# Small loads on ACT's queue, w_mod products between the transposes, two rows as single-column matmuls

## The chip, the core and the metric

The kernel runs on one core of one Trainium2 chip. The metric is the device time of one execution in microseconds (us), here the median of 3 runs. The core has a matrix engine (TensorE, in the profile PE, with its weight loads shown as PEld), two elementwise engines (VectorE = DVE, ScalarE = ACT), GpSimd (POOL, almost unused here) and SyncE (SP). SP and ACT can both issue DMA transfers; each engine goes through its instructions in program order.

## The reference

Two layers of a mixer on x of 256 tokens by 2048 channels, batch 1. What matters for this change is the very beginning of layer 0:

```
c_act = silu(c)
mod = c_act @ w_mod[0] + b_mod[0]            # 2048 -> 3 * 2048
shift, scale, gate = split(mod, 3)
h = rms_norm(x, g_norm) * (1 + scale) + shift
proj = h @ w_in[0]                           # 2048 -> 15424
```

Behind it come retention, latent attention, their projections, the merge, the output projection, the second layer with the same shapes, and a last RMS norm. All of it is float32.

## The kernel before, in words

Tokens are 256, so one operand of the large products is always 256 columns wide or two blocks of 128 rows. Weights stream once from memory in pieces of 128 x 1024 (512 KB). Each piece is split by ACT (`hi`, L240) and DVE (`lo`, L241) into two float32r parts, and three matmuls (hi·hi, hi·lo, lo·hi; L273 and L276) replace one float32 product.

The change lies in the opening stretch, `start()` (L510 to L559) and the loads ahead of it (L164 to L205). `start()` makes the first four of sixteen 128-row blocks of h, so that the first columns of w_in can be multiplied before the rest of w_mod has been read. Its steps:

- Small loads: the constants `cst` (identity and tables, 67 KB, L165), five row vectors `rows` (b_mod, g_norm, g_cq, g_ckv, c; L182) that PE turns into columns (L185), and `posi`, the positions broadcast to 128 partitions (L197). SiLU of c gives `cact` (L194).
- x in four tiles of 512 KB (`xin`, L205), each squared and summed by ACT (L518). DVE makes the rotary angles from `posi` (L216 to L224). Then the reciprocal root (L305 to L310).
- PE transposes x in eight pairs of blocks (L530), and ACT copies each pair from a PSUM buffer into `xT` (L532). Four such buffers (`aux_tile`) rotate.
- `spread` (L327 to L337) turns the reciprocal root into a row `r` on all partitions, and DVE scales four blocks of x with it (`xh0`, L444).
- The first 512 columns of shift and scale take sixteen pieces of w_mod (`wmod`, 512 KB, two 128-row blocks each), loaded with the scale half first (L391). The scale half is multiplied on PE with `cact` as the stationary operand, one result row of 512 columns (L540, sixteen matmuls). The shift half is accumulated on DVE, one instruction for each block of rows (L347, L349, sixteen in all), and PE then sums over the partitions with a vector of ones (`mod_sum`, L355).
- `make_amul` (L424) forms (1 + scale)·g; DVE multiplies xh0 by it (L549); ACT adds the shift and rounds (`hi`, L556), DVE makes `lo` (L557). With that PE starts on w_in (L273).

In `start()` the order on PE, DVE and ACT is the order of the code (`manual_schedule`). Elsewhere a scheduler chooses. DMA transfers carry one of eight completion semaphores, DMAHW0 to DMAHW7, handed out in rotation over all queues in the order in which the scheduler takes the transfers; a transfer that gets a semaphore again waits, on its own queue, until the earlier one that carried it has landed.

Of the kernel before, what the change touches and what calls it, by code (L numbers as in the profile page):

```python
# [13 lines left out]
AF = mybir.ActivationFunctionType  # L14
ALU = mybir.AluOpType
AX = mybir.AxisListType

P = 128
S = 256
D = 2048  # L20
KT = D // P
# [87 lines left out]
def trunk(ctx: ExitStack, tc: tile.TileContext, x, c, positions, w_mod, b_mod, g_norm, w_in, g_cq,  # L109
          g_ckv, w_uq, w_ukv, w_ret_proj, w_mla_proj, w_out, g_final, consts, decay, out):  # L110
    nc = tc.nc
    V, A, T, DMA = nc.vector, nc.scalar, nc.tensor, nc.sync
# [14 lines left out]
    def aux_tile():  # L127
        return paux.tile([P, 512], F32, name="aux", tag="aux")

    def tmp_tile():  # L130
        return tp.tile([P, 512], F32, name="tmp", tag="tmp")

    def small(n):
        return sp.tile([P, 16], F32, name="small", tag="small")[:, :n]

    def quarter(name, dtype=F32):
        return big.tile([P, 1024], dtype, name=name, tag="quarter")

    def blocks(name):

        return quarter(name).rearrange("p (a b) -> p a b", b=S)
# [20 lines left out]
            return [u[:, kt % 2, cols] for u in self.pair(kt // 2)]  # L162

    cst = cp.tile([P, K_COLS], F32, name="cst")  # L164
    DMA.dma_start(cst, consts)  # L165
    ident = cst[:, K_ID : K_ID + P]
    ones = cp.tile([P, P], F32, name="ones")
    V.memset(ones, 1.0)
# [6 lines left out]
    def vectors(l):  # L175
        rows = tp.tile([P, P], F32, name="rows", tag="tmp")
        put = [(b_mod[l], 48), (g_norm[l], 16), (g_cq[l], 4), (g_ckv[l], 4)]
        if l == 0:
            put.append((c[0], 16))
        r0 = 0  # L180
        for src, n in put:
            DMA.dma_start(rows[r0 : r0 + n, :], src.rearrange("(r q) -> r q", q=P))  # L182
            r0 += n
        ps = aux_tile()
        T.transpose(ps[:, :r0], rows[:r0, :], ident[:r0, :r0])  # L185
        V.tensor_copy(vec[l][:, :r0], ps[:, :r0])

    vectors(0)
    bm = [v[:, 0:48] for v in vec]
    gn = [v[:, 48:64] for v in vec]  # L190
    gcq = [v[:, 64:68] for v in vec]
    gckv = [v[:, 68:72] for v in vec]
    cact = cp.tile([P, KT], F32, name="cact")
    A.activation(cact, vec[0][:, 72:88], AF.Silu)  # L194

    posi = tp.tile([P, S], I32, name="posi", tag="tmp")
    DMA.dma_start(posi, positions.broadcast_to([P, S]))  # L197
    pos = dp.tile([P, S], F32, name="pos", tag="dtab")


# [60 lines left out]
    def mm3(o, a, b, start, stop):  # L261

        T.matmul(o, a[0], b[0], start=start, stop=False, skip_group_check=True)  # L263
        T.matmul(o, a[0], b[1], start=False, stop=False, skip_group_check=True)  # L264
        T.matmul(o, a[1], b[0], start=False, stop=stop, skip_group_check=True)  # L265
# [36 lines left out]
    def rsqrt_small(v, n):  # L302

        s, y, t = small(n), small(n), small(n)
        A.activation(s, v, AF.Sqrt)  # L305
        V.reciprocal(y, s)
        V.tensor_tensor(t, y, y, ALU.mult)
        V.tensor_tensor(t, t, v, ALU.mult)
        V.tensor_scalar(t, t, -0.5, 1.5, ALU.mult, ALU.add)
        V.tensor_tensor(y, y, t, ALU.mult)  # L310
        return y
# [16 lines left out]
    def spread(y, r=None):  # L328

        tt = tmp_tile()  # L330
        pr = aux_tile()
        for t in range(2):
            V.tensor_scalar(tt[:, t * P : (t + 1) * P], ident, y[:, t : t + 1], None, ALU.mult)
            T.matmul(pr[:, t * P : (t + 1) * P], ones, tt[:, t * P : (t + 1) * P], start=True, stop=True)
        r = tt[:, S : 2 * S] if r is None else r
        A.activation(r, pr[:, :S], AF.Copy)
        return r  # L337

    mods = [cp.tile([P, 48 if l < DEPTH - 1 else 32], F32, name=f"mod{l}") for l in range(DEPTH)]
    amul = [cp.tile([P, KT], F32, name=f"amul{l}") for l in range(DEPTH)]  # L340
# [3 lines left out]
    def mod_rows(acc, w, k0, nk):  # L344
        for k in range(nk):
            if k0 + k == 0:
                V.tensor_scalar(acc, w[:, k, :], cact[:, 0:1], None, ALU.mult)  # L347
            else:
                V.scalar_tensor_tensor(acc, w[:, k, :], cact[:, k0 + k : k0 + k + 1], acc, ALU.mult, ALU.add)  # L349

    def mod_sum(l, m0, ng, pieces, one):
        ps = aux_tile()
        for b in range(ng):
            for i, piece in enumerate(pieces):
                T.matmul(ps[:, b : b + 1], piece[:, b * P : (b + 1) * P], one, start=i == 0, stop=i == len(pieces) - 1)  # L355
        V.tensor_tensor(mods[l][:, m0 : m0 + ng], ps[:, :ng], bm[l][:, m0 : m0 + ng], ALU.add)
# [29 lines left out]
    def mod_fetch(w, l, m0, k0, ng):  # L386

        n = ng * P
        w = w.rearrange("p (k n) -> p k n", n=n)
        nd = 1024 // n  # L390
        DMA.dma_start(w, w_mod[l, k0 * P : (k0 + nd) * P, m0 * P : m0 * P + n].rearrange("(k p) n -> p k n", p=P))  # L391
        return w
# [30 lines left out]
    def make_amul(l, k, n):  # L423
        V.scalar_tensor_tensor(amul[l][:, k : k + n], mods[l][:, 16 + k : 16 + k + n], 1.0,  # L424
                               gn[l][:, k : k + n], ALU.add, ALU.mult)
# [17 lines left out]
    def normalise(dst, k, r):  # L443
        V.tensor_tensor(dst, xT[:, k : k + 2, :], r.unsqueeze(1).broadcast_to([P, 2, S]), ALU.mult)  # L444
        return dst
# [60 lines left out]
    def start():  # L506

        ng = GROUPS[0][0][1]
        nd = 8 // ng
        ws = {(i, k): mod_fetch(quarter("wmod"), 0, 16 * i, k, ng) for i in (1, 0) for k in range(0, KT, nd)}  # L510
        ss = small(4).rearrange("p (q t) -> p q t", q=2)
        extra, room = quarter("extra"), quarter("room")
        row, acc = extra[:, : ng * P], extra[:, 512 : 512 + ng * P]
        xh0, hh = blocks("xh0"), Pairs("h")
        with tc.manual_schedule(engines={ENG.PE, ENG.DVE, ENG.Activation}):
            for q in range(2):
                for t in range(2):
                    A.activation(room, xin[t][q], AF.Square, accum_out=ss[:, q, t : t + 1])  # L518
            rotary = rotary_tables(quarter("angle"))
            next(rotary)  # L520
            v = small(2)
            V.tensor_tensor(v, ss[:, 0, :], ss[:, 1, :], ALU.add)
            V.tensor_scalar(v, v, 1.0 / D, EPS, ALU.mult, ALU.add)
            y = rsqrt_small(v, 2)
            for pair in range(KT // 2):
                ps = aux_tile()
                for a in range(2):
                    for t in range(2):
                        f = (2 * pair + a) * P
                        T.transpose(ps[:, a * S + t * P : a * S + (t + 1) * P],  # L530
                                    xin[t][f // 1024][:, f % 1024 : f % 1024 + P], ident)
                A.activation(xT[:, 2 * pair : 2 * pair + 2, :].rearrange("p a b -> p (a b)"), ps, AF.Copy)  # L532
            r = spread(y, dp.tile([P, S], F32, name="r0", tag="dtab"))
            for k in range(0, ng, 2):
                normalise(xh0[:, k : k + 2, :], k, r)
            next(rotary, None)
            pr = aux_tile()
            for k0 in range(0, KT, nd):
                for k in range(nd):
                    T.matmul(pr[0:1, : ng * P], cact[:, k0 + k : k0 + k + 1], ws[1, k0][:, k, :], start=k0 + k == 0,  # L540
                             stop=k0 + k == KT - 1)
            for k0 in range(0, KT - nd, nd):
                mod_rows(acc, ws[0, k0], k0, nd)
            A.activation(row[0:1, :], pr[0:1, : ng * P], AF.Copy)
            mod_sum(0, 16, ng, [row[0:1, :]], ones[0:1, 0:1])
            make_amul(0, 0, ng)
            mod_rows(acc, ws[0, KT - nd], KT - nd, nd)
            for k in range(ng):
                V.tensor_scalar(xh0[:, k, :], xh0[:, k, :], amul[0][:, k : k + 1], None, ALU.mult)  # L549
            first = [w_in[0, k0 * P : (k0 + 2) * P, n : n + 512] for n in (C_RQ, C_RK) for k0 in range(0, ng, 2)]  # L550
            prepared.append(load_split(first[0], 2, 512, early=True))
            mod_sum(0, 0, ng, [acc], ones[:, 0:1])
            for k in range(ng):
                hi, lo = hh.block(k)
                shift = mods[0][:, k : k + 1]
                A.activation(hi, xh0[:, k, :], AF.Identity, bias=shift)  # L556
                V.scalar_tensor_tensor(lo, xh0[:, k, :], shift, hi.bitcast(F32), ALU.add, ALU.subtract)  # L557
            prepared.extend(load_split(src, 2, 512, early=True) for src in first[1:HP])
        return r, hh  # L559
# [444 lines left out]
    r = u = None  # L1004
    for l in range(DEPTH):
        r, u = layer(l, r, u)
# [22 lines left out]
```

## Time and profile before

| what | value |
|---|---|
| median of 3 runs | 2056.74 us (2056.7 to 2057.08) |
| profiled execution | 2057.32 us |
| its span, first to last instruction | 2055.5 us |
| PE busy | 2025.8 us, 99% of the span |
| DVE, ACT busy | 1483.6 us (72%), 1061.7 us (52%) |
| first w_in matmul | 39.93 us after the start of the span |

The span is one execution as the hardware profiler saw it; 1.8 us of the execution lie outside it. A busy share is an average over the whole span, so what happens in its first 45 us has to be read from the timeline of that stretch, and the granted clock from the table of stretches.

### The profile page before, as it was taken

The numbers are of one execution on the slowest core, as the hardware profiler recorded it, in microseconds if no ns is written. First come the engines' busy times: TensorE is split into PE (matmuls) and PEld (weight loads), VectorE is DVE, ScalarE is ACT, GpSimd is POOL, SyncE is SP. The second block draws the span as 40 slices with busy tenths as digits, with TensorE's granted clock in tenths as the row PEclk, the third lists the DMA queues.
The fourth block names the chain that finished last, engine by engine and source line by source line (L and its number), as shares of the span: only waits on it lengthen the run. The fifth ranks groups of instructions, "written<-read, shape, count | busy, mean of one in ns | idle before, by whom it ended". The sixth has DMA issues, their size and how long they took to land.

```text
span 2055.5 us, 31773 instructions
## 1 busy us (share of the span) xinstructions
PE 2025.8 (99%) x12414; PEld 1802.8 (88%) x12414; DVE 1483.6 (72%) x2082; ACT 1061.7 (52%) x1489; POOL 0.2 (0%) x4
## 2 busy tenths in 40 slices
PE   7999999999999999999999999999999999999998
PEld 4888888998899998889998888889889999988887
DVE  5799986778777777775577776568776877765574
ACT  4554355654456664444454464456544666644453
POOL 0000000000000000000000000000000000000000
PEclk9999999999999999999999999999999999999999
DMA  8998966567866668875569966665677666666572
GB/s 315 321 310 274 308 198 194 159 191 259 302 191 195 195 187 274 281 267 185 182 196 333 326 209 189 194 180 156 198 238 223 205 185 195 208 224 192 190 243 90
DMA packets 251222, 460.59 MB, mean 224 GB/s; under 512 B 18464, under 2 KB 68032, under 8 KB 251072
## 3 DMA queue, kind: packets, MB, share of 16 engines
q1 hardware_dynamic: 251072, 458.57, 69.8%
q8 instruction: 97, 1.59, 0.3%
q14 instruction: 53, 0.43, 0.1%
HBM read 456.41 MB, written 2.10 MB: 223 GB/s over the span
## 4 chain that ended last, share of the span: by engine, by line
PE 94%; DMA 3%; DVE 2%; ACT 1%; issue 1%; SPq 0%; ACTq 0%; DVEq 0%
PE acc L273 57%; PE acc L276 28%; DMA ring<-in_w_mod 2%; DMA wmod<-in_w_mod 1%; PE aux L264 1%; PE aux L265 1%; PE aux L263 1%; PE acc L263 1%; PE acc L264 1%; PE acc L265 1%; DVE extra L349 0%; PE aux L880 0%; ACT whl L240 0%; PE aux L721 0%; PE aux L846 0%
## 5 line engine op out<-in xcount | busy, mean ns | idle before, releaser
L240 ACT ACTIVATE whl<-wst 128x1024 fp32r<-128x1024 f32 (+1 forms) x708 | 709.0, 1007 | 805.0 <-PE acc L276 699.1
L241 DVE TENSOR_TENSOR whl<-wst,whl 128x1024 fp32r<-128x1024 f32 (+1 forms) x708 | 814.2, 1156 | 378.3 <-ACT whl L240 374.3
L273 PE MATMUL acc<-whl,h 128*128 128x512 f32 x2048 | 515.4, 392 | 0.0
L273 PEld LDWEIGHTS acc<-whl,h 128*128 128x128 f32 x2048 | 381.4, 188 | 77.1
L273 PE MATMUL acc<-h,whl 128*128 128x256 f32 x2432 | 328.1, 285 | 4.0 <-ACT h L240 2.4
L273 PEld LDWEIGHTS acc<-h,whl 128*128 128x128 f32 x2432 | 307.8, 192 | 6.3 <-ACT h L240 3.2
L276 PE MATMUL acc<-whl,h 128*128 128x512 f32 x1024 | 279.6, 392 | 0.4 <-DVE whl L241 0.4
L273 PE MATMUL acc<-whl,z 128*128 128x512 f32 x1024 | 254.8, 390 | 1.2 <-ACT whl L240 1.2
L273 PEld LDWEIGHTS acc<-whl,z 128*128 128x128 f32 x1024 | 191.8, 188 | 41.1 <-ACT whl L240 1.6
L276 PEld LDWEIGHTS acc<-whl,h 128*128 128x128 f32 x1024 | 190.9, 188 | 39.4 <-DVE whl L241 1.0
L276 PE MATMUL acc<-h,whl 128*128 128x256 f32 x1216 | 176.3, 284 | 0.0
L276 PEld LDWEIGHTS acc<-h,whl 128*128 128x128 f32 x1216 | 158.7, 192 | 0.1
L276 PE MATMUL acc<-whl,z 128*128 128x512 f32 x512 | 137.1, 390 | 0.0
L400 DVE SCALAR_TENSOR_TENSOR macc<-ring,cact,macc 128x1024 f32<-128x1024 f32 x75 | 96.1, 1281 | 35.7 <-DMA ring<-in_w_mod 35.2
L400 DVE SCALAR_TENSOR_TENSOR macc<-wst,cact,macc 128x1024 f32<-128x1024 f32 x90 | 115.0, 1278 | 0.0
L276 PEld LDWEIGHTS acc<-whl,z 128*128 128x128 f32 x512 | 96.0, 188 | 20.1 <-DVE whl L241 0.2
L273 PE MATMUL acc<-c,whl 128*128 128x256 f32 x640 | 100.2, 288 | 0.0
L273 PEld LDWEIGHTS acc<-c,whl 128*128 128x128 f32 x640 | 85.9, 191 | 0.2
L273 PE MATMUL acc<-m,whl 128*128 128x256 f32 x512 | 67.3, 283 | 0.0
L273 PEld LDWEIGHTS acc<-m,whl 128*128 128x128 f32 x512 | 64.0, 192 | 0.1
L276 PE MATMUL acc<-c,whl 128*128 128x256 f32 x320 | 57.6, 285 | 0.0
L273 PE MATMUL acc<-whl,m 128*128 128x512 f32 (+1 forms) x256 | 56.5, 365 | 0.0
(256 smaller groups left out, 1880.1 us busy)
## 6 DMA issues: line engine op xcount, KB each, us to landing
wst<-in_w_in SPq DMA_DIRECT2D x416, 512.0 KB, 4.4
wst<-in_w_mod SPq DMA_DIRECT2D x96, 512.0 KB, 4.7
ring<-in_w_mod SPq DMA_DIRECT2D x80, 512.0 KB, 5.3
wst<-in_w_ret_proj SPq DMA_DIRECT2D x64, 512.0 KB, 4.8
wst<-in_w_mla_proj SPq DMA_DIRECT2D x64, 512.0 KB, 4.4
wst<-in_w_out SPq DMA_DIRECT2D x64, 512.0 KB, 3.7
wst<-in_w_ukv SPq DMA_DIRECT2D x32, 512.0 KB, 4.3
wst<-in_w_uq SPq DMA_DIRECT2D x32, 384.0 KB, 4.2
```

The costliest lines, as they stand in the source:

```text
L240: A.activation(hi, src, AF.Copy)
L241: return V.tensor_tensor(lo, src, hi.bitcast(F32), ALU.subtract)
L263: T.matmul(o, a[0], b[0], start=start, stop=False, skip_group_check=True)
L264: T.matmul(o, a[0], b[1], start=False, stop=False, skip_group_check=True)
L265: T.matmul(o, a[1], b[0], start=False, stop=stop, skip_group_check=True)
L273: T.matmul(o, x, y, start=start and i == 0, stop=False, skip_group_check=True)
L276: T.matmul(o, x, y, start=False, stop=stop, skip_group_check=True)
L400: V.scalar_tensor_tensor(macc, w, cact[:, k : k + 1], macc, ALU.mult, ALU.add)
```

## The change

Three things change. The constants, the five row vectors of layer 0 and the positions are issued by ACT, and SP begins with x. Eight of the sixteen scale products move up between the last four pairs of transposes; the PSUM buffer of their sum is therefore held from before the first pair. DVE's shift rows stop after fourteen of sixteen, the scale is applied to xh0 after ten of them, and the last two rows are multiplied on PE, with the 128 x 128 blocks of w_mod as the stationary operand and one column of `cact` moving, into the same PSUM columns as the sum over partitions.

```
-    DMA.dma_start(cst, consts)
+    A.dma_start(cst, consts)
...
-            DMA.dma_start(rows[r0 : r0 + n, :], src.rearrange("(r q) -> r q", q=P))
+            (DMA if l else A).dma_start(rows[r0 : r0 + n, :], src.rearrange("(r q) -> r q", q=P))
...
-    DMA.dma_start(posi, positions.broadcast_to([P, S]))
+    A.dma_start(posi, positions.broadcast_to([P, S]))
...
+            pr = aux_tile()
+
+            def scale_rows(k0):
+                for k in range(k0, k0 + nd):
+                    T.matmul(pr[0:1, : ng * P], cact[:, k : k + 1], ws[1, k0][:, k - k0, :], start=k == 0, stop=k == KT - 1)
+
             for pair in range(KT // 2):
...
+                if pair >= KT // 4:
+                    scale_rows((pair - KT // 4) * nd)
...
-            pr = aux_tile()
-            for k0 in range(0, KT, nd):
-                for k in range(nd):
-                    T.matmul(pr[0:1, : ng * P], cact[:, k0 + k : k0 + k + 1], ws[1, k0][:, k, :], start=k0 + k == 0,
-                             stop=k0 + k == KT - 1)
+            for k0 in range(KT // 4 * nd, KT, nd):
+                scale_rows(k0)
             for k0 in range(0, KT - nd, nd):
                 mod_rows(acc, ws[0, k0], k0, nd)
-            A.activation(row[0:1, :], pr[0:1, : ng * P], AF.Copy)
-            mod_sum(0, 16, ng, [row[0:1, :]], ones[0:1, 0:1])
-            make_amul(0, 0, ng)
-            mod_rows(acc, ws[0, KT - nd], KT - nd, nd)
-            for k in range(ng):
-                V.tensor_scalar(xh0[:, k, :], xh0[:, k, :], amul[0][:, k : k + 1], None, ALU.mult)
+                if k0 == KT // 2:
+                    A.activation(row[0:1, :], pr[0:1, : ng * P], AF.Copy)
+                    mod_sum(0, 16, ng, [row[0:1, :]], ones[0:1, 0:1])
+                    make_amul(0, 0, ng)
+                    for k in range(ng):
+                        V.tensor_scalar(xh0[:, k, :], xh0[:, k, :], amul[0][:, k : k + 1], None, ALU.mult)
...
-            mod_sum(0, 0, ng, [acc], ones[:, 0:1])
+            ps = aux_tile()
+            for b in range(ng):
+                T.matmul(ps[:, b : b + 1], acc[:, b * P : (b + 1) * P], ones[:, 0:1], start=b == 0, stop=False,
+                         skip_group_check=True)
+            for k in range(KT - nd, KT):
+                for b in range(ng):
+                    T.matmul(ps[:, b : b + 1], ws[0, KT - nd][:, k - KT + nd, b * P : (b + 1) * P], cact[:, k : k + 1],
+                             start=False, stop=k == KT - 1, skip_group_check=True)
+            V.tensor_tensor(mods[0][:, 0:ng], ps[:, :ng], bm[0][:, 0:ng], ALU.add)
```

The head of ACT's instructions after the change, with the semaphores that each waits for (before, ACT began with the table load, and the seven transfers stood first on SP without a wait):

```order
L165 DMA cst<-in_consts 128x134
L182 DMA rows<-in_b_mod 48x128
L182 DMA rows<-in_g_norm 16x128
L182 DMA rows<-in_g_cq 4x128
L182 DMA rows<-in_g_ckv 4x128 [waits DMAHW1_49]
L182 DMA rows<-in_c 16x128 [waits DMAHW3_49]
L197 DMA posi<-in_positions 128x256 [waits DMAHW5_49]
L194 ACT_TABLE_LOAD
L194 ACTIVATE cact<-vec_88 128x16 [waits DVE_49]
```

The seven transfers moved from SP to ACT. The rotation now runs over both queues: cst has DMAHW0, the first tile of x DMAHW1, the second DMAHW2, b_mod DMAHW3, the third tile DMAHW4, g_norm DMAHW5, the fourth tile DMAHW6, g_cq DMAHW7, the first piece of w_mod DMAHW0, and g_ckv, the tenth transfer, DMAHW1 again.

PE from its first instruction to the first w_in matmuls, before:

```order
L185 MATMUL aux<-cst,rows 128x88
L530 MATMUL aux<-cst,xin 128x128 x32
L334 MATMUL aux<-tmp,ones 128x128 x2
L540 MATMUL aux<-wmod,cact 1x512 x16
L355 MATMUL aux<-ones,extra 128x1 x8
L273 MATMUL acc<-h,whl 128x256 x16
```

The same stretch of PE after:

```order
L536 MATMUL aux<-cst,xin 128x128 x20
L529 MATMUL aux<-wmod,cact 1x512 x2
L536 MATMUL aux<-cst,xin 128x128 x4
L529 MATMUL aux<-wmod,cact 1x512 x2
L334 MATMUL aux<-tmp,ones 128x128 x2
L529 MATMUL aux<-wmod,cact 1x512 x8
L355 MATMUL aux<-ones,extra 128x1 x4
L559 MATMUL aux<-ones,extra 128x1 x4
L563 MATMUL aux<-cact,wmod 128x1 x8
L273 MATMUL acc<-h,whl 128x256 x16
```

The four transposes and two products alternate four times in all. Eight scale products moved ahead of the two matmuls of `spread` (L334), and eight single-column matmuls (L563) came in between the sum over partitions (L559) and w_in.

DVE from `xh0` to the first `lo` of h, before:

```order
L444 TENSOR_TENSOR xh_157<-xT,r_236 128x512 x2
L347 TENSOR_SCALAR extra<-wmod,cact 128x512
L349 SCALAR_TENSOR_TENSOR extra<-wmod,cact,extra 128x512 x13
L356 TENSOR_TENSOR mod_117<-aux,vec_88 128x4
L424 SCALAR_TENSOR_TENSOR amul_119<-mod_117,vec_88 128x4
L349 SCALAR_TENSOR_TENSOR extra<-wmod,cact,extra 128x512 x2
L549 TENSOR_SCALAR xh_157<-xh_157,amul_119 128x256 x4
L241 TENSOR_TENSOR whl<-wst,whl 128x1024
L557 SCALAR_TENSOR_TENSOR h<-xh_157,mod_117,h 128x256 x4
```

The same stretch of DVE after:

```order
L444 TENSOR_TENSOR xh_157<-xT,r_245 128x512 x2
L347 TENSOR_SCALAR extra<-wmod,cact 128x512
L349 SCALAR_TENSOR_TENSOR extra<-wmod,cact,extra 128x512 x9
L356 TENSOR_TENSOR mod_117<-aux,vec_88 128x4
L424 SCALAR_TENSOR_TENSOR amul_119<-mod_117,vec_88 128x4
L554 TENSOR_SCALAR xh_157<-xh_157,amul_119 128x256 x4
L349 SCALAR_TENSOR_TENSOR extra<-wmod,cact,extra 128x512 x4
L241 TENSOR_TENSOR whl<-wst,whl 128x1024
L565 TENSOR_TENSOR mod_117<-aux,vec_88 128x4
```

The scale products of xh0 moved ahead of the last four rows, and two rows are gone. Behind `start()` no engine's order differs.

## Rows read from the trace of the kernel before

**Rows 1.** Table of stretches: the whole core from 40 us on (columns named)

```profile
core 0: us, PE busy (x) PEld busy (x) DVE busy (x) ACT busy (x) POOL busy (x), PEclk, DMA share, GB/s
40.00:2055.50 2015.50, 2000.59 (x12329) 1790.08 (x12329) 1460.17 (x2032) 1043.97 (x1460) 0.00 (x0) 1.00 0.70 222
```

**Rows 2.** Timeline, SP's transfers: start, length of the issue, engine, what

```profile
2.50 0.25 SPq L182 DMA_DIRECT2D rows<-in_g_ckv  x1
2.79 0.32 SPq L182 DMA_DIRECT2D rows<-in_c  x1
3.15 0.42 SPq L197 DMA_DIRECT2D posi<-in_positions  x1
3.62 2.16 SPq L205 DMA_DIRECT2D xin<-in_x  x4
```

**Rows 3.** Waits of the transfer queue, first 110 us: total, times, longest

```profile
SPq L391 <- DMA xin<-in_x: 2.0, 4, 0.6
```

**Rows 4.** Timeline, small loads to first copy into xT; brackets: idle before

```profile
4.49 0.38 PE L185 MATMUL aux<-cst,rows 88*128 88x88 f32 x1 [4.49 <-DMA rows<-in_c]
5.19 0.22 ACT L194 ACTIVATE cact<-vec 128x16 f32<-128x16 f32 x1 [3.19 <-DVE vec L186]
7.17 0.29 DVE L216 CAST pos<-posi 128x256 f32<-128x256 int32 x1 [2.01 <-DMA posi<-in_positions]
8.47 1.06 ACT L518 ACTIVATE room<-xin 128x1024 f32<-128x1024 f32 x1 [3.06 <-DMA xin<-in_x]
12.70 0.43 DVE L224 TENSOR_SCALAR angle<-angle 128x512 f32<-128x512 f32 x1
13.54 1.28 ACT L305 ACT_TABLE_LOAD   x1
13.76 0.17 DVE L523 TENSOR_SCALAR small<-small 128x2 f32<-128x2 f32 x1
14.95 3.24 ACT L532 ACTIVATE xT<-aux 128x512 f32<-128x512 f32 x6
```

**Rows 5.** Landing times of the row vectors, over the whole span

```profile
DMA to landing us min/median/max: 1.6/3.1/4.6
```

**Rows 6.** Timeline, transposes to DVE's first shift rows

```profile
15.58 3.66 PE L530 MATMUL aux<-cst,xin 128*128 128x128 f32 x16 [2.35 <-ACT xT L532]
19.61 13.89 PE L540 MATMUL aux<-wmod,cact 128*1 128x512 f32 x32
20.18 1.29 DVE L444 TENSOR_TENSOR xh<-xT,r 128x512 f32<-128x512 f32 x2 [3.63 <-ACT r L336]
24.51 0.49 DVE L347 TENSOR_SCALAR extra<-wmod,cact 128x512 f32<-128x512 f32 x1 [3.04 <-DMA wmod<-in_w_mod]
25.94 9.42 DVE L349 SCALAR_TENSOR_TENSOR extra<-wmod,cact,extra 128x512 f32<-128x512 f32 x12 [0.16 <-DMA wmod<-in_w_mod]
```

**Rows 7.** Timeline, six later transposes of the same shape

```profile
694.24 0.82 PE L880 MATMUL aux<-cst,sm 128*128 128x128 f32 x6
```

**Rows 8.** Timeline, last shift rows to the first w_in matmuls

```profile
35.55 1.53 DVE L349 SCALAR_TENSOR_TENSOR extra<-wmod,cact,extra 128x512 f32<-128x512 f32 x2
36.99 1.14 DVE L549 TENSOR_SCALAR xh<-xh,amul 128x256 f32<-128x256 f32 x4
37.22 1.83 PE L355 MATMUL aux<-ones,extra 128*128 128x1 f32 x8 [1.99 <-DVE extra L349]
39.93 3.56 PE L273 MATMUL acc<-h,whl 128*128 128x256 f32 x16 [0.87 <-ACT h L556]
44.28 2.08 PE L273 MATMUL acc<-h,whl 128*128 128x256 f32 x16
47.16 2.08 PE L273 MATMUL acc<-h,whl 128*128 128x256 f32 x16
```

**Rows 9.** Table of stretches around them (columns as in Rows 1)

```profile
37.00:40.00 3.00, 1.91 (x9) 1.85 (x9) 2.42 (x8) 0.63 (x2) 0.00 (x0) 0.50 1.05 388
```

**Rows 10.** Groups of PE by line and shape, 400 us on: total busy, mean ns

```profile
L319 PE MATMUL aux<-ones,tmp 128*128 128x1 f32 x32 | 3.8, 240 | 0.0
```

## The prediction

> **What bounds the kernel now.** I read the table of stretches first. From 40 us to the end PE is busy for 2000.6 of 2015.5 us [rows 1], so behind `start()` nothing but PE's own work matters, and no engine's order changes there. What the change can move is the moment at which PE begins on w_in, 39.93 us [rows 8]. A microsecond there should come through whole: the transfers behind it wait for splits that wait for PE.
>
> Then I read the timeline of the first 45 us for what ends last at each step. Four steps follow each other. The small loads and x bring ACT to its first copy into xT at 14.95 us [rows 4]. PE's transposes and `spread` let DVE make xh0 at 20.18, but w_mod holds DVE until 24.51 [rows 6]. DVE's sixteen shift rows run to 35.55 + 1.53 = 37.08, and a short tail on PE leads to 39.93 [rows 8].
>
> The sum is made against the profiled execution: span 2055.5 us plus 1.8 us around it, 2057.32, which is 0.58 us above the median.
>
> **Step 1, loads on ACT's queue.** SP issued x from 3.62 us on, and ACT could use the first tile at 8.47, 4.85 us later [rows 2, 4]. With x first on SP, at about 0.7 us, it lands at about 5.6. But g_ckv gets the semaphore of that first tile, so ACT stands still until 5.6, and c, posi, the table load, `cact` and the squares stand behind it. That such a wait is real shows in SP's waits for x before w_mod, four of them [rows 3].
>
> From 5.6: g_ckv 0.25 us, c, then posi, which starts 0.65 us behind g_ckv as before, at 6.26 [rows 2]. For c I take the landing of before, from 2.79 at issue to 4.49 at PE, 1.70 us [rows 2, 4]: 5.9 + 1.7 = 7.6, `cact` at 8.3, squares at about 8.55, no later than before. Posi took 3.15 to 7.17, 4.0 us [rows 2, 4], and so arrives at 10.26. DVE's angles then need 7.17 to 13.13, 5.96 us [rows 4]; they end at 16.2, and the two small sums ahead of the root stand behind them on DVE, another 0.4 us with their waits. Root and first copy come at 16.75 instead of 14.95: **+1.8 us**. The angles, idle cover before, are now the late side.
>
> The bounds: if posi took 2 us, ACT's squares would decide and the term be 0. Row vectors loaded in mid-stream landed in up to 4.6 us against 1.6 at best [rows 5]; 3 us more on posi makes +4.8. The value is that of the same load.
>
> The Trainium skill ("DMA: Bandwidth & Descriptors", "Queues, rings and completion order") says that each DMA engine takes turns between queues, a packet at a time. By that the small loads pass most of the x and w_mod already outstanding on SP, and the term stays near +1.8; if they waited for it, the upper end would hold. No row here has two queues in use, so this trace can't say.
>
> **Step 2, eight products between transposes.** All of these stand before `spread`, so before r, xh0 and the first shift row. Before, PE began its second half of transposes 0.63 us after ACT's first copy (15.58) [rows 4, 6]. Now pr holds one of four buffers, so three pairs go ahead and five, 20 transposes, come after the first copy, with eight products, 16 records on PE, between them.
>
> Prices: a record of the product is 13.89 / 32 = 0.43 us [rows 6]. A transpose took 3.66 / 16 = 0.229 us here, where the granted clock prints 1.00, but 0.11 at 694 us ((0.82 - 0.27) / 5) [rows 6, 7]; so I read the opening as the lower level, 1.2 GHz, whatever the column says. Of the new stretch I take as much at the lower level as those 3.66 us before: eight transposes (1.83) and 1.6 us of products (under two records at double price), then 14 records (6.0) and 12 transposes at 0.11 (1.3). That is 10.8; 0.4 more because the pause ahead of it is longer. 11.2 us. All at the high level would be 9.1, all at the low one 18.3.
>
> From the end of the transposes to the end of xh0 took 19.24 to 21.47, 2.23 us [rows 6]. So the first shift row starts at 16.75 + 0.63 + 11.2 + 2.25 = 30.8 instead of 24.51: +6.3, of which 1.8 is step 1's, **+4.5** this step's. w_mod, which landed at 24.51 before, is there by then. Nothing is won behind it: the remaining eight products (6.9 us) end at 36, beside DVE's rows.
>
> **Step 3, DVE.** Before, 24.51 to 37.08, 12.57 us. Now one row at 0.52 with its gap, nine at 0.785 (9.42 / 12), 0.2 for modulation and amul (35.36 to 35.55), four scalings of xh0 (1.14, behind the rows before, now ahead of the last four), four rows (3.14): 12.07 us [rows 6, 8]. **-0.5**: two rows leave, four scalings take their place.
>
> **Step 4, the tail.** The sum over partitions waits for DVE's last row, and the eight new matmuls stand behind it on PE although their data came long before. Four matmuls were eight records in 1.83 us [rows 8], at granted clock 0.50, the lower level [rows 9]. Twelve are 24 records: 5.5 us there. At the higher level a record of this shape costs 3.8 / 32 = 0.12 [rows 10], 2.9 us in all. PE is idle for some 5 us ahead of it, against 2 before, so it starts low; I let it rise late in the stretch and take 4.9. **+3.05** (+1.0 to +3.7).
>
> **Step 5, the first w_in chunk.** Before it took 39.93 to 44.28, 4.35 us; the next takes 2.88 [rows 8]. Part of that was the low clock. After a longer busy tail it may be over: **-0.7** (-1.4 to 0).
>
> **Sum**: 1.8 + 4.5 - 0.5 + 3.05 - 0.7 = +8.15. 2057.32 + 8.15 - 0.58 = 2064.9 us in terms of the median. w_in starts at about 48.9.
>
> **The rivals.**
>
> *The queue does not hold.* ACT's seven transfers go out by 3.6 us, and step 1 gives x's whole 2.9 us instead of +1.8. For it: x does go out 2.9 us earlier. Against: the wait on the first tile's semaphore stands in ACT's rows. Steps 2 to 5 stay: 8.15 - 1.8 - 2.9 = +3.45, 2060.2 us.
>
> *The small loads starve.* From 5.6 us on c and posi share 16 DMA engines with a full stream of x and w_mod, in which row vectors took up to 4.6 us [rows 5]. Step 1 becomes +4.8, and the longer pause keeps PE low for another microsecond or so: +12, 2068.8 us.
>
> *Not slower: x's early start carries through.* Place: PE from the first copy to the tail. If ACT is not held and PE works at the higher level throughout, step 1 is -2.9, step 2 +2.4, step 3 -0.5, step 4 +1.0, step 5 -1.4: -1.4, 2055.3 us. It decides only if both hold at once; against it is the transposes' 0.229 us [rows 6] and the clock of 0.50 ahead of w_in [rows 9].
>
> **How the numbers follow.** Forecast 0.55, starving 0.17, queue not holding 0.17, early start 0.07, the rest unnamed. A measurement here can tell 0.2%, 4.1 us. The forecast, from +4 to +12 with its bounds taken together, lies almost wholly above; starving does; of the queue that doesn't hold a good third does. That makes slower 0.80, same 0.17, faster 0.03: even the best sum gains 1.4 us. The range, 2059.0 to 2069.2, takes in the queue that doesn't hold and most of starving and leaves out the early start.
>
> **What would show it.** Step 1: ACT's g_ckv issue at 5 to 6 us behind three that went out at once, the cast of pos at about 10.3, the first copy into xT at about 16.8; a cast before 7 proves it wrong. Step 2: the first shift row at about 31, right behind xh0 and with no wait for w_mod. Step 3: 12 us from it to the last row. Step 4: 24 records of single-column matmuls for 4 to 5.5 us ahead of the first h, w_in at 48 to 49.5. The whole is wrong if w_in starts before 42 us, or if a shift of w_in's start doesn't reach the end.

## The result and the profile after

The changed kernel takes 2070.04 us, the median of 5 runs (2068.97 to 2071.85), against 2057.08 (2056.7 to 2059.07) for the kernel before: a ratio of 1.0062, 95% interval 1.0051 to 1.0073, so 10.5 to 15 us slower. The forecast was 2064.9 us, in a range up to 2069.2. The direction held, and every term but the last has the forecast sign; the size was too small, most of all in step 1. The profiled execution, the fastest of the five, has a span of 2067.2 us, 11.7 more than before.

The timeline of the changed kernel's opening, from the small loads to the first copy into xT, with rows left out at each "..."; the columns are start, length, engine, instruction, and in brackets the idle time before it with its releaser. These rows answer to [rows 2, 4].

```profile
0.73 1.81 SPq L205 DMA_DIRECT2D xin<-in_x  x4
...
1.16 0.45 ACTq L182 DMA_DIRECT2D rows<-in_b_mod  x1
...
2.11 0.57 ACTq L182 DMA_DIRECT2D rows<-in_g_cq  x1
...
4.51 0.26 ACTq L182 DMA_DIRECT2D rows<-in_g_ckv  x1
...
6.72 0.40 ACTq L182 DMA_DIRECT2D rows<-in_c  x1
...
7.26 0.36 ACTq L197 DMA_DIRECT2D posi<-in_positions  x1
...
11.40 0.38 PE L185 MATMUL aux<-cst,rows 88*128 88x88 f32 x1 [11.40 <-DMA rows<-in_c]
...
11.57 3.37 PE L536 MATMUL aux<-cst,xin 128*128 128x128 f32 x16
...
12.22 1.04 ACT L518 ACTIVATE room<-xin 128x1024 f32<-128x1024 f32 x1
...
13.14 0.29 DVE L216 CAST pos<-posi 128x256 f32<-128x256 int32 x1 [1.07 <-DMA posi<-in_positions]
...
16.92 1.28 ACT L305 ACT_TABLE_LOAD   x1
...
18.67 0.43 DVE L224 TENSOR_SCALAR angle<-angle 128x512 f32<-128x512 f32 x1
...
19.51 2.53 ACT L538 ACTIVATE xT<-aux 128x512 f32<-128x512 f32 x5
```

ACT's queue stops twice: before g_ckv, until x's first tile is there (4.51), and again before c, until b_mod is (6.72). c then reaches PE at 11.40 and the positions DVE at 13.14. The angles end at 19.10, so the first copy, right behind the root, comes at 19.51 instead of 14.95. x's first tile was there at about 4.5 and waited. The late c alone would have cost most of this: the squares behind it begin at 12.22 instead of 8.47, and ACT's table load behind them ends at 18.20, so without the angles the first copy could have come at about 18.3 (an estimate from these rows).

The same timeline from there to w_in, answering to [rows 6, 8]:

```profile
20.15 1.12 PE L536 MATMUL aux<-cst,xin 128*128 128x128 f32 x4 [5.20 <-ACT xT L538]
...
21.19 3.57 PE L529 MATMUL aux<-wmod,cact 128*1 128x512 f32 x4
...
24.69 0.69 PE L536 MATMUL aux<-cst,xin 128*128 128x128 f32 x4
...
25.31 1.88 PE L529 MATMUL aux<-wmod,cact 128*1 128x512 f32 x4
...
33.07 1.29 DVE L444 TENSOR_TENSOR xh<-xT,r 128x512 f32<-128x512 f32 x2 [11.96 <-ACT r L336]
...
34.28 0.48 DVE L347 TENSOR_SCALAR extra<-wmod,cact 128x512 f32<-128x512 f32 x1
...
43.21 3.11 DVE L349 SCALAR_TENSOR_TENSOR extra<-wmod,cact,extra 128x512 f32<-128x512 f32 x4
...
46.46 1.84 PE L559 MATMUL aux<-ones,extra 128*128 128x1 f32 x8 [5.16 <-DVE extra L349]
...
48.16 3.55 PE L563 MATMUL aux<-cact,wmod 128*128 128x1 f32 x16
...
52.51 3.55 PE L273 MATMUL acc<-h,whl 128*128 128x256 f32 x16 [0.80 <-ACT h L569]
...
56.85 2.08 PE L273 MATMUL acc<-h,whl 128*128 128x256 f32 x16
```

DVE waits for r alone, 11.96 us, and w_mod has long been there. The first two products between transposes take 3.57 us, the next two 1.88: the clock rose between them. The tail is 24 single-column records in a row, 5.25 us from 46.46 to 51.71. The first w_in matmul starts at 52.51, 12.58 us later than before.

The table of stretches of the changed kernel, columns as in [rows 1]: the pause ahead of the second half of the transposes, the first two products, the pause ahead of the tail, the end of the tail, the start of w_in, and the rest.

```profile
18.00:20.00 2.00, 0.00 (x0) 0.00 (x0) 1.63 (x6) 0.80 (x4) 0.00 (x0) 0.50 1.04 385
...
22.00:24.00 2.00, 2.00 (x4) 0.25 (x2) 0.00 (x0) 0.04 (x1) 0.00 (x0) 0.50 1.05 387
...
44.00:46.00 2.00, 0.00 (x0) 0.00 (x0) 1.93 (x3) 0.00 (x0) 0.00 (x0) 0.50 0.00 0
...
50.00:52.00 2.00, 1.71 (x9) 1.63 (x8) 0.16 (x1) 0.05 (x1) 0.00 (x0) 0.50 0.27 101
52.00:54.00 2.00, 1.49 (x6) 1.47 (x7) 1.51 (x4) 2.00 (x5) 0.00 (x0) 0.50 0.00 0
...
52.00:2067.00 2015.00, 2000.08 (x12329) 1790.31 (x12329) 1461.03 (x2032) 1044.53 (x1461) 0.00 (x0) 1.00 0.70 222
```

The granted clock is at its lower level, 0.50, in both pauses and in what follows each of them. In the last row PE is busy for 2000.08 of 2015 us, as in [rows 1]: the loss lies in the opening. Of the 12.6 us 0.9 come back by 121 us: before, PE lost 0.8 us between 80 and 97 us, mostly to a split that it now finds ready.

### The profile page after: what moved, and what is told of

Read it like the earlier page. It is cut to its first block, busy times and chain, and to the rows that moved or that the text cites. A ratio compares the mean times of both kernels' runs of the same rounds, so it can differ in the third digit from the quotient of the medians.

```text
span 2067.2 us, 31801 instructions
## 1 busy us (share of the span) xinstructions
PE 2029.4 (98%) x12430; PEld 1804.7 (87%) x12430; DVE 1482.8 (72%) x2080; ACT 1061.5 (51%) x1489; POOL 0.2 (0%) x4
## 4 chain that ended last, share of the span: by engine, by line
PE 96%; DVE 2%; ACT 1%; DMA 1%; issue 0%; ACTq 0%
PE acc L273 58%; PE acc L276 29%; PE aux L264 1%; PE aux L265 1%; PE aux L263 1%; PE acc L263 1%; PE acc L264 1%; PE acc L265 1%; PE aux L893 0%; DVE extra L349 0%; PE aux L529 0%; PE aux L734 0%; PE aux L859 0%; PE aux L860 0%; PE aux L920 0%
## 5 line engine op out<-in xcount | busy, mean ns | idle before, releaser
L273 PE MATMUL acc<-whl,h 128*128 128x512 f32 x2048 | 515.4, 392 | 0.0
L273 PEld LDWEIGHTS acc<-whl,h 128*128 128x128 f32 x2048 | 381.4, 188 | 77.0
L273 PE MATMUL acc<-h,whl 128*128 128x256 f32 x2432 | 328.0, 285 | 3.9 <-ACT h L240 2.5
L273 PEld LDWEIGHTS acc<-h,whl 128*128 128x128 f32 x2432 | 307.7, 192 | 6.2 <-ACT h L240 3.2
L273 PE MATMUL acc<-whl,z 128*128 128x512 f32 x1024 | 254.8, 390 | 1.2 <-ACT whl L240 1.2
L273 PEld LDWEIGHTS acc<-whl,z 128*128 128x128 f32 x1024 | 191.8, 188 | 41.1 <-ACT whl L240 1.6
L273 PE MATMUL acc<-c,whl 128*128 128x256 f32 x640 | 100.2, 288 | 0.0
L273 PEld LDWEIGHTS acc<-c,whl 128*128 128x128 f32 x640 | 85.9, 191 | 0.2
L273 PE MATMUL acc<-m,whl 128*128 128x256 f32 x512 | 67.3, 283 | 0.0
L273 PEld LDWEIGHTS acc<-m,whl 128*128 128x128 f32 x512 | 64.0, 192 | 0.1
L273 PE MATMUL acc<-whl,m 128*128 128x512 f32 (+1 forms) x256 | 56.5, 365 | 0.0
```

Source lines behind the costliest of these rows:

```text
L273: T.matmul(o, x, y, start=start and i == 0, stop=False, skip_group_check=True)
```

## The experiments

Each run is compared with runs of the kernel before on the same chip. "w_in" is the start of the first L273 matmul in the run's profile, "chunk" the time from it to the second group of sixteen (4.35 us before). The first four take the change apart.

**Loads alone.** The kernel before with the small loads on ACT:

```
-    DMA.dma_start(cst, consts)
+    A.dma_start(cst, consts)
-            DMA.dma_start(rows[r0 : r0 + n, :], src...)
+            (DMA if l else A).dma_start(rows[r0 : r0 + n, :], src...)
-    DMA.dma_start(posi, positions.broadcast_to([P, S]))
+    A.dma_start(posi, positions.broadcast_to([P, S]))
```

> Only the seven small loads move to ACT's queue. Theory (the loads land late because they share the transfer engines with x, and ACT stands behind two of them): c lands near 11.3 us and posi near 13.1 as in the changed kernel, the first copy into xT comes at about 19.5 instead of 14.95, the products on PE end 4.6 us later than 33.50, DVE waits for them, and w_in starts at about 44.5 (39.93 before): +4.5 us, about 2061.3. Rival (the whole loss comes from what PE does, the loads are hidden by the wait for w_mod at 24.51): w_in at 40 to 41.5, under 2059.

Measured 2062.81 us, ratio 1.0025 (1.0016 to 1.0035). Its timeline:

```profile
19.85 3.23 ACT L532 ACTIVATE xT<-aux 128x512 f32<-128x512 f32 x6
...
24.94 14.06 PE L540 MATMUL aux<-wmod,cact 128*1 128x512 f32 x32
...
26.68 0.48 DVE L347 TENSOR_SCALAR extra<-wmod,cact 128x512 f32<-128x512 f32 x1
...
45.42 3.88 PE L273 MATMUL acc<-h,whl 128*128 128x256 f32 x16 [0.87 <-ACT h L556]
```

The first copy is as late as in the changed kernel, and the products on PE end 5.5 us later than before. w_in is 5.5 us late, a microsecond more than expected. The theory stands; DVE's wait for w_mod does not hide it, because the scale's products and not the first shift row decide.

**Products between the transposes alone** (loads on SP, DVE's sixteen rows and the tail as before):

```
+                if pair >= KT // 4:
+                    scale_rows((pair - KT // 4) * nd)
...
+            for k0 in range(KT // 4 * nd, KT, nd):
+                scale_rows(k0)
```

> Only the eight scale products move between the last four pairs of transposes; loads on SP, sixteen shift rows on DVE, tail as before. Theory (they stand before r and hence before DVE's first shift row, at the lower clock in part): first copy into xT at 14.95 as before, first shift row at about 28.8 to 29.5 instead of 24.51, w_in at 44.2 to 45: +4.3 to +5 us, about 2061.5. Rival (they fill time in which PE waited anyway, since DVE waits for w_mod until 24.51): first shift row still at 24.5, w_in at 39.9, no change.

Measured 2061.35 us, ratio 1.0019 (1.001 to 1.0029):

```profile
14.73 2.53 ACT L538 ACTIVATE xT<-aux 128x512 f32<-128x512 f32 x5
...
29.01 0.48 DVE L347 TENSOR_SCALAR extra<-wmod,cact 128x512 f32<-128x512 f32 x1
...
44.30 3.88 PE L273 MATMUL acc<-h,whl 128*128 128x256 f32 x16 [0.87 <-ACT h L561]
```

The first shift row is 4.5 us late and w_in 4.4. The rival, that the products fill idle time, falls.

**Two rows on PE alone:**

```
-            mod_rows(acc, ws[0, KT - nd], KT - nd, nd)
...
-            mod_sum(0, 0, ng, [acc], ones[:, 0:1])
+            (the four sums, then the eight single-column matmuls, as in the change)
```

> Only the last two shift rows move from DVE to PE, behind the sum over partitions; loads on SP, products behind spread, xh0 scaled after fourteen rows. Theory (12 matmuls in a row are 24 records, 0.12 us each at the higher clock and 0.23 at the lower, against 8 before, and DVE saves 1.57 us): DVE's last row at about 35.4, w_in at 39.1 to 41.1, -0.8 to +1.2 us, within what can be told from no change. Rival (the single-column matmuls alone cost the whole 3.3 us that the tail grew by): w_in at 42 or later.

Measured 2058.35 us, ratio 1.0005 (0.9995 to 1.0014), w_in at 40.80, the chunk 5.4 us: nothing that can be told from no change, as expected. The rival falls: the eight matmuls cost 3.55 us and save DVE 1.6, but here xh0's scaling runs beside them. In the changed kernel the scaling stands ahead of the last rows, and DVE ends only 0.5 us sooner.

**Everything but the loads:**

```
-    A.dma_start(cst, consts)
+    DMA.dma_start(cst, consts)
...
```

> The changed kernel with the small loads back on SP. Theory (the loads' share is the shift of the first copy into xT, 4.56 us): first copy at 14.95, the rest as in the changed kernel, 33.0 us from there to w_in, so w_in at about 48, +8 us, about 2065. Rival (with w_mod not yet there the products wait on PE for it, so that the loads' delay cost nothing): w_in at 51 to 52.5, +12 us as with all three.

Measured 2066.15 us, ratio 1.0041 (1.0026 to 1.0055), first copy at 14.68, w_in at 48.17, 8.2 us late. The loads' share in the whole is therefore 52.51 - 48.17 = 4.3 us, about the 4.8 by which their first copy is later.

The next four ask why the loads cost so much, and whether the change can be mended.

**No wait on ACT's queue.** Only four small loads on ACT, none with a semaphore already used; the gains go behind x on SP:

```
+    A.dma_start(cst, consts)
...
+    A.dma_start(rows0[48:64, :], c[0]...)
+    A.dma_start(posi, positions.broadcast_to([P, S]))
+    A.dma_start(rows0[0:48, :], b_mod[0]...)
...
+    for r0, src, n in ((0, g_norm[0], 16), (16, g_cq[0], 4), (20, g_ckv[0], 4)):
+        DMA.dma_start(rowsg[r0 : r0 + n, :], src...)
```

> The kernel before, with x first on SP and only four small loads on ACT's queue (constants, c, positions, b_mod), so that none takes a semaphore again and ACT never stands still; the three gain vectors go on SP behind x and are turned into columns later. Theory (two causes of about the same size: ACT stood behind x's first tile and behind b_mod, and every small load takes 4.5 to 6 us beside the stream of x instead of 1.5 to 4): c lands at 6 to 6.5, b_mod and positions at 7 to 8, the first squares come at 8.4 to 8.8 and the first copy into xT at 14.8 to 15.3, no earlier than the 14.95 of before although x lands at about 4.5; w_in at 39 to 40.5, no change (2055.5 to 2058). Rival (the semaphores alone): c lands by 3.5 and positions by 6, squares start with x at about 4.6 to 5, first copy at 11.5 to 12.5, w_in 2 to 3 us earlier.

Measured 2059.39 us, ratio 1.0014 (1.0005 to 1.0023). Its timeline, and from the view of b_mod's line its one landing time:

```profile
2.12 0.45 ACTq L193 DMA_DIRECT2D rows<-in_b_mod  x1
...
8.82 0.29 DVE L231 CAST pos<-posi 128x256 f32<-128x256 int32 x1 [7.68 <-DMA posi<-in_positions]
...
9.67 0.34 PE L195 MATMUL aux<-cst,rows 64*128 64x64 f32 x1 [9.67 <-DMA rowsg<-in_g_norm]
...
16.48 3.24 ACT L547 ACTIVATE xT<-aux 128x512 f32<-128x512 f32 x6
```

```profile
DMA to landing us min/median/max: 7.4/7.4/7.4
```

Nothing stands still on ACT, and c, positions and b_mod are issued by 2.6 us. Yet b_mod lands 7.4 us after its issue, the positions 7.2 us after theirs, against 4.0 before, and PE gets the vectors at 9.67 instead of 4.49. (The releaser named there, g_norm, isn't read by this matmul; b_mod is the last that is.) The first copy comes 1.5 us later than before and w_in, at 42.21, 2.3 us later, where 39 to 40.5 was expected. The rival falls; of the theory the slow landing holds, and its price was put too low. In the changed kernel itself the positions go out 4.1 us later than before (7.26 against 3.15) and need 1.9 us more from there to DVE (5.88 against 4.02); 1.4 us of the two together stayed hidden, since the angles had that much time to spare before. So the standing queue is the larger part there: ACT stands 1.8 us for x's first tile and 1.95 us for b_mod. How much each would cost without the other isn't shown, since this run also issues the loads in another order.

**The changed kernel with the eight matmuls ahead of the sum:**

```
+            (the eight L563 matmuls, start on the first)
             first = [w_in[0, ...
...
+            (the four L559 matmuls, stop on the last)
```

> The changed kernel with the eight single-column matmuls ahead of the four that sum over the partitions, on PE. Theory (they stand behind a wait for DVE's last row that they don't need): they run at about 41.3 to 45 beside DVE's rows, and from DVE's last row to w_in it takes 2.9 us again instead of 6.2; w_in at about 49.2 instead of 52.5, about 2066.7. Rival (the tail is long because of the lower clock, wherever they stand): w_in at 51.5 or later.

Measured 2066.97 us, ratio 1.005 (1.0037 to 1.0064), 3 us less than the changed kernel (2066.16 to 2068.16 against 2068.97 to 2071.85):

```profile
42.30 2.41 PE L558 MATMUL aux<-cact,wmod 128*128 128x1 f32 x16
...
47.45 1.86 PE L563 MATMUL aux<-ones,extra 128*128 128x1 f32 x8 [2.73 <-DVE extra L349]
...
50.10 3.88 PE L273 MATMUL acc<-h,whl 128*128 128x256 f32 x16 [0.79 <-ACT h L569]
```

The eight run beside DVE's last rows. From DVE's last row, 47.39, to w_in it takes 2.7 us. The theory stands: the same work in the other order makes a short tail. What the low clock added to the long one is seen in the run with wide matmuls, below.

**The same tail in the kernel before:**

```
-            mod_rows(acc, ws[0, KT - nd], KT - nd, nd)
+            (the eight single-column matmuls, then the four sums)
```

> The kernel before with the last two shift rows on PE in that better order, and nothing else changed. Theory: DVE's last row ends at 35.2 instead of 37.1, the eight matmuls run at 35.2 to 37.5 on PE (they come right behind the sum of the scale, itself done at 35.2), then the sum; the tail is a little hidden: w_in at 39 to 40.8, within 0.2% of before (2056 to 2058). Rival (DVE's two rows are worth their 1.6 us): w_in at 38.2, 2055.

Measured 2058.02 us, ratio 1.0005 (0.9996 to 1.0014). w_in is at 40.26 and the chunk takes 5.3 us. Inside what was expected, but not for the reason: the scale's products ended 1.2 us later than before, with the same code ahead of them (their records take 14.68 us instead of 13.89, as if the clock rose later), and the granted clock is at 0.50 through nearly the whole chunk.

**Small loads over both queues, ahead of x, with that tail:**

```
-            DMA.dma_start(rows[r0 : r0 + n, :], src...)
+            (A if l == 0 and i in (1, 2, 3) else DMA).dma_start(rows[r0 : r0 + n, :], src...)
-    DMA.dma_start(posi, positions.broadcast_to([P, S]))
+    A.dma_start(posi, positions.broadcast_to([P, S]))
```

> As the run before (last two rows on PE ahead of the sum), and the small loads split over both queues ahead of x: constants, b_mod and c on SP, then x; g_norm, g_cq, g_ckv and positions on ACT, none with a semaphore that was used. Theory (a load issued before x lands fast; x and w_mod come 1.7 us earlier, since SP issues four loads less): c lands at about 3.5 to 4.5, positions at 6 to 7, x's first tile at about 6.8, w_mod's first shift piece at about 22.8 instead of 24.5, w_in 1.5 us earlier than in the run before, 2055 to 2056. Rival (the loads on ACT, beside x, land late again and hold the vectors): c's column and the squares come later than 8.5 us, w_in 1 to 3 us later than before.

Measured 2056.48 us, ratio 0.9998 (0.9989 to 1.0007):

```profile
1.65 0.41 SPq L182 DMA_DIRECT2D rows<-in_c  x1
...
2.06 0.37 ACTq L197 DMA_DIRECT2D posi<-in_positions  x1
...
3.62 0.38 PE L185 MATMUL aux<-cst,rows 88*128 88x88 f32 x1 [3.62 <-DMA rows<-in_c]
...
6.01 0.29 DVE L216 CAST pos<-posi 128x256 f32<-128x256 int32 x1 [1.73 <-DMA posi<-in_positions]
...
23.43 0.49 DVE L347 TENSOR_SCALAR extra<-wmod,cact 128x512 f32<-128x512 f32 x1 [3.10 <-DMA wmod<-in_w_mod]
...
34.02 2.75 PE L552 MATMUL aux<-cact,wmod 128*128 128x1 f32 x16
...
39.27 1.10 PE L273 MATMUL acc<-h,whl 128*128 128x256 f32 x3 [0.80 <-ACT h L563]
```

The loads theory holds. Issued ahead of x, which SP begins to issue at 2.10, c is on PE 2.0 us after its issue and the positions on DVE 3.95 us after theirs, although those come from ACT's queue, and w_mod comes 1.1 us sooner. So it is the stream ahead of a load that delays it, not the second queue; the 4.6 us of [rows 5] was a load on SP's own queue behind weights. In time nothing is gained that can be told from no change: w_in starts 0.7 us sooner, but the chunk takes 5.4 us. The table of stretches of this run:

```profile
34.00:35.00 1.00, 1.00 (x10) 0.99 (x10) 0.93 (x5) 0.72 (x1) 0.00 (x0) 0.97 1.03 381
...
42.00:45.00 3.00, 3.00 (x16) 3.00 (x16) 1.76 (x2) 0.36 (x2) 0.00 (x0) 0.50 0.37 85
```

PE runs single-column matmuls without a gap from 33.04 on, and the clock falls in the midst of them, to 0.50 from 35 us on, and stays low to 45 us, through nearly the whole first chunk.

The last three test whether the low clock is what tail and chunk cost too much, by keeping PE busy with wide matmuls whose results nobody reads, where it waits anyway.

```
+        def warm(n, cols):
+            pw = aux_tile()
+            for _ in range(n):
+                T.matmul(pw[:, :cols], ones, xT[:, 0:2, :]...[:, :cols], start=True, stop=True)
...
+            warm(1, 256)                        # ahead of the copy of the scale's row
...
+            warm(2, 512)                        # behind the sum of the scale; 5 in the changed kernel
...
+            warm(1, 256)                        # behind the tail
```

In the changed kernel:

> The changed kernel with idle gaps of PE ahead of the tail filled by matmuls whose result nobody reads (one of 256 columns while ACT copies the scale's row, five of 512 columns while PE would wait for DVE's last row, one of 256 columns ahead of w_in). Theory (what the tail and the first chunk cost above their price at the higher level is the clock, which falls in that gap): the granted clock stays at 1.00 until the tail, 24 records take 2.9 to 4 us instead of 5.4, the first chunk 2.9 to 3.5 instead of 4.34; w_in at 50 to 51, end 2.5 to 3.9 us earlier than the changed kernel, about 2066.5. Rival (single-column matmuls are as slow with the clock up): tail and chunk as in the changed kernel, 2069 to 2070.

Measured 2067.29 us, ratio 1.0049 (1.0036 to 1.0063), 2.8 us less than the changed kernel (2066.84 to 2068.1 against 2068.97 to 2071.85):

```profile
45.28 1.02 PE L567 MATMUL aux<-ones,extra 128*128 128x1 f32 x8 [0.67 <-DVE extra L349]
...
46.16 1.93 PE L571 MATMUL aux<-cact,wmod 128*128 128x1 f32 x16
...
48.89 3.42 PE L273 MATMUL acc<-h,whl 128*128 128x256 f32 x16 [0.26 <-ACT h L578]
...
53.64 2.08 PE L273 MATMUL acc<-h,whl 128*128 128x256 f32 x16
```

```profile
46.00:49.00 3.00, 2.74 (x22) 2.34 (x22) 0.56 (x3) 0.68 (x2) 0.00 (x0) 1.00 0.47 127
...
50.00:53.00 3.00, 3.00 (x17) 3.00 (x16) 2.54 (x4) 1.93 (x3) 0.00 (x0) 0.50 0.01 4
```

Half of the theory holds: with the clock at 1.00 the same 24 records take 2.8 us instead of 5.25, and from DVE's last row to w_in it takes 3.8 us instead of 6.2. (1.2 us of the earlier w_in have another reason: the first shift row, ahead of any added matmul, is at 33.10, since with the same code the first copy came 0.4 us sooner and the first two products took 2.79 us instead of 3.57.) The other half falls: the clock fell behind the tail instead of ahead of it, at 50 us, and the first chunk took 4.75 us, more than before.

In the kernel before, and in the kernel before with the loads split:

> The kernel before with such unread matmuls in PE's gaps ahead of w_in (256 columns, then two of 512, then 256). Theory: the clock stays up, the last sum takes 1 us instead of 1.83, w_in still starts at 39.9 (DVE's split ends at 39.26 and holds the modulation), the first chunk takes 2.9 instead of 4.35: -1.4 us, 2055.3. Rival (the clock falls anyway, a little later, and stays down longer into w_in): 0 to +1 us.

> The same, with the small loads split over both queues ahead of x as two runs ago. Theory: the first shift row at 23.4 instead of 24.5, w_in at 38.9, first chunk 2.9: -2.5 us, 2054.3, the best so far. Rival: the clock falls anyway and only the 1.1 us of the loads are left, 2055.7.

Measured 2057.55 us, ratio 1.0001 (0.9992 to 1.001), and 2056.25 us, ratio 0.9993 (0.9984 to 1.0002). Both rivals: in the first the sum takes 1.02 us, but w_in is at 39.78 and the chunk takes 4.38, for the clock falls between 39 and 40; in the second w_in is at 39.90, because the scale's products ended at 33.5 instead of 32.4 in the run with the loads split (14.55 us of records instead of 13.89, as if the clock rose later), and the chunk takes 4.75. No version was shown to beat the kernel before; this one is the nearest.

## Why the prediction fell short

*Step 1 is the term that was mis-sized*: +1.8 forecast, 19.51 - 14.95 = +4.56 measured. It took the landing times of before for c (1.70 us) and the positions (4.0). c took 4.7 from issue to PE and the positions 5.9. And it counted only the wait for x's first tile, as if b_mod, whose semaphore c gets, were there by then; b_mod had needed 5.5 us, and c went out at 6.72 instead of 5.9. The first tile itself came sooner than forecast, 4.5 instead of 5.6. Of the 2.8 us that the term lacked, the positions' later issue is 1.0 and their slower landing 1.9. c was late too, against the forecast: the squares began at 12.22, not at 8.55. The upper bound of +4.8 had the size, and so the rival of the starving loads came nearest, with 2068.8 us; it deserved more than 0.17. In part that was luck: it charged 3 us to the landing of the positions, which took 1.9 more, and did not have the wait for b_mod. The changed kernel without the loads on ACT, 4.3 us earlier at w_in, shows the price; the runs with four loads on ACT and with the loads ahead of x show the slow landing beside x. How the price divides between that and the waits for shared semaphores stays open.

The Trainium skill ("DMA: Bandwidth & Descriptors", "Queues, rings and completion order") has each DMA engine take turns between queues, a packet at a time. I read that as small loads passing x. The runs go against that reading: behind x on the other queue a load of 8 to 24 KB took 4.5 to 7.4 us, where one issued ahead of x took 1.5 to 2.0. They don't show in what turns the engines served the queues.

*Step 2* was +4.5 and measured 34.28 - 24.51 - 4.56 = +5.2. The products stand before r, as forecast, with no wait for w_mod. The stretch was made up otherwise, and errors cancel in part. The text ahead of the prediction has pr's buffer held from before the first pair, and I took three pairs to go ahead of the first copy; sixteen transposes, four pairs, ran there at 11.57, as before, so sixteen came behind it and not twenty. At the lower level I charged eight transposes and under two records of products; it was four transposes and four records (3.57 us). And at the higher level four transposes between products took 0.6 us (24.69 to 25.31) where I took 0.44. Alone this change measured +4.5 at the first shift row.

*Step 3*, 12.07 us forecast: 34.28 to 46.32, 12.04. Right.

*Step 4* was +3.05 and measured 52.51 - 46.32 = 6.19 against 2.85, +3.34. The clock stayed low through all 24 records, 5.25 us; the choice of 4.9 us between the levels was too kind. That the order behind the sum makes it long was right, as the swapped tail shows.

*Step 5* was -0.7 and measured 0: 4.34 us. The clock was still low behind the single-column records, 0.50 at 52 to 54 us.

The measured terms add to 4.56 + 5.2 - 0.53 + 3.34 + 0 = 12.57 us at w_in, of which 11.7 reach the end of the span. Of the 4.4 us by which the sum falls short there, step 1 has 2.8, steps 2 and 5 0.7 each, and step 4 0.3. The 0.9 that come back make it 3.5; the rest of the distance from 2064.9 to 2070.04 us is that the changed kernel's profiled execution, 2068.97, lies 1.1 under its median, where the one before lay 0.6 above. The rivals of the unheld queue and of the early start fall: even without any wait on ACT the first copy came later than before.

Still open: the executions of one kernel differ by up to 3 us (2056.1 to 2059.2 for the kernel before), and in the profiles the clock rises and falls at other times with the same code up to there (the scale's products end at 33.50 in the kernel before and at 34.65 with only the tail changed). Whether the two belong together was not tried. Why a small load lands so late beside the stream isn't shown either.

## What to carry to other kernels

A small load that the opening needs belonged ahead of the big ones here, on whichever queue; a second queue did not carry it past the running stream, and the compute engine that issued it stood behind the semaphores it shared with that stream. Work moved into an engine's idle time can cost in full if it stands ahead of what the next engine waits for, so look for what ends last at that place, not for the gap. Put operands that are ready ahead of those that wait, and measure changes of clock on the stretch behind them.

## What the runs showed of the hardware that was not expected

Single-column matmuls with new weights each time took 0.12 us a record at the higher level and 0.22 to 0.23 at the lower, as the rows of before had it. What was new: the clock fell while PE ran nothing but these, back to back (at 35 us in the run with the loads on both queues), and was still low after 5.25 us of them in the changed kernel. In the kernel before the granted clock prints 1.00 up to 36 us, although the transposes at 15.58 take 0.229 us each, twice what they take later; before its first printed change the column can't be taken for the level. And landing under load was longer than any row of before had shown: 7.4 us for 24 KB.
